# Start addresses of the matmul operands: from multiples of 64 bytes to multiples of 128 bytes

## The chip, the cores and the metric

The kernel runs on one core of a Trainium2 chip. The metric is the device time of one execution in microseconds (us). Before the change it is 881.71 us, the median of three runs (881.45 to 884.4).

## The reference

Two transformer blocks, one after the other, on 256 tokens of width 1024, all in float32:

```python
def reference(x, mem, ...):
    x = first_block(x, mem, ...)    # differential + stick-breaking attention, cross attention, MLP
    return second_block(x, ...)     # compressed/selected/window attention + dilated attention, gates, MLP

# both blocks end in an MLP of this form (d_ff = 4096)
a = jnp.square(jax.nn.relu(rms_norm(h, g_mlp) @ w_up))
h = h + a @ w_down
```

Nearly all the arithmetic is in the products with weight matrices: `w_in`, `w_out`, `w_xq`, `w_xkv`, `w_xo`, `w_up`, `w_down` of the first block and their counterparts in the second.

## The kernel before

**Layout.** Activations stay in the on-chip memory (SBUF) transposed, 128 features on the partitions and 256 tokens along the row, eight such slices to a tile: `[128, 8, 256]` float32, 8,192 bytes per partition. There are eight buffers of that size (class `c8` of `t`), and with the tiles of the MLP's hidden units (`mhl`, also 8,192 bytes) they hold every activation that a large product reads.

**Products in three parts.** Each float32 operand of a large product is split in a high and a low part of type float32r: ScalarE writes the high part (`hi = Copy(x)`) and VectorE the low one (`lo = x - hi`). `mm3` (lines 263 to 268) then issues three matmuls into the same PSUM bank: high weight with high activation (L266), low weight with high activation (L267), high weight with low activation (L268). In `gemm_t` and in the MLPs the weights are the stationary operand (128 x 128) and the activations the moving one (256 columns, 1,024 bytes per partition). In `gemm_n` (L319 to L321) it is the other way round: 128 tokens of the activation are stationary and 256 columns of weights move. `acc_add` has the same three parts in another order (L334, L335, L338). The built program has 1,544 matmuls of each of L266 to L268, 432 of each of L319 to L321 and 80 of each of L334, L335 and L338: 6,168 in all. The rest (attention scores and values, transposes) are plain float32.

**Weights.** `wunit` (line 207) brings a unit of weights with DMAs from SyncE's queue into staging buffers `wraw` and splits it piece by piece: 512 numbers per partition go to one buffer of `whi` (L232, ScalarE) and one of `wlo` (L233, VectorE). Each of the two has NPART = 8 buffers that are used in turn, and each buffer has STEP floats more than its 512:

```python
    NRAW, NPART, NP = 6, 8, 10
    STEP = 16
...
hi, lo = [self.t([P, 512 + self.STEP], tag, self.NPART, F32R, self.wp)[:, :rows * cols] ...
          for tag in ("whi", "wlo")]
```

One pair of buffers feeds 12 matmuls in a row, in `gemm_t` (two slices of 128 weight rows, two groups of 128 columns, three parts) and in the MLP's second product (`out_rows`, one weight row slice, four column groups, three parts). One turn of the MLP's loop (`mlp`, `for u in range(2, nu)`) is one unit of `w_up` (four pairs, 48 matmuls, into bank G) and one of `w_down` (four pairs, 48 matmuls, into banks Z and X): 96 matmuls and each of the eight pairs once.

**Where the operands stand.** The constants come first in memory, one tile after the other, each rounded up to 32 bytes; `gsub`, 4 bytes, is one of the first. The pool with the activations follows, then the pool of the weights. The built program's map has these start addresses (bytes within a partition):

| buffers | before | remainder |
|---|---|---|
| eight buffers of activations, `mhl` among them | 30784 + 8192 i | 64 by 1024 |
| `whi` | 194368 + 2112 i | 320, 384, 448, 0, 64, 128, 192, 256 by 512 |
| `wlo` | 211264 + 2112 i | the same eight by 512 |
| `wraw` | 169792 + 4096 i | 64 by 256 |

Rows inside a buffer begin at multiples of 512 bytes from its start. So before the change every operand of a large product starts at a multiple of 64 bytes: all activations at an odd one (64 past a multiple of 128), half of the weight buffers at an odd one and half at an even one. In the stretches that the rows below show, the pairs are used in this order (remainder by 512 of `whi` / `wlo`):

| runs of 12 that start at | pairs in turn |
|---|---|
| 300.29 to 310.15 us, first MLP | 192/192, 256/256, 128/384, 384/448, 448/0, 0/128, 64/64, 320/320 |
| 742.39 to 752.35 us, second MLP | 192/192, 0/128, 256/256, 64/64, 320/320, 128/384, 384/448, 448/0 |
| 518.45 and 519.86 us, `gemm_n` | 192/192, 256/256 |

Of the kernel before, what the change touches and what calls it, by code (L numbers as in the profile page):

```python
# [9 lines left out]
F32 = mybir.dt.float32  # L10
# [7 lines left out]
P = 128  # L18
# [116 lines left out]
class Builder:  # L135
# [66 lines left out]


    NRAW, NPART, NP = 6, 8, 10
    STEP = 16

    def wunit(self, src, j, n, dmas=1, before=None, hold_lo=None):

# [17 lines left out]
        for j0 in range(0, j, rows):  # L226
            for c0 in range(0, n, cols):
                hi, lo = [self.t([P, 512 + self.STEP], tag, self.NPART, F32R, self.wp)[:, :rows * cols].rearrange(
                    "p (r c) -> p r c", r=rows) for tag in ("whi", "wlo")]
# [200 lines left out]
    def setup(self):  # L430
        nc, I = self.nc, self.I
        nc.scalar.preload_act_table_set(MAIN_SET)
        self.ones = self.cp.tile([P, P], F32, name="ones")
        nc.vector.memset(self.ones, 1.0)

        z = self.Z()
        for _ in range(10):
            nc.tensor.matmul(z[:, 0:P], self.ones, self.ones, start=True, stop=True)
        gains = self.const("gains", [P, 7 * 8 + 1], eng=nc.scalar)
        self.xT = self.t([P, KC, T], "h")  # L440
        xv = I["xT"].rearrange("(k p) t -> p k t", p=P)
        self.first_unit = self.wcols(I["w_in"], 1536, dmas=4, before=lambda i: nc.sync.dma_start(
            self.xT[:, 2 * i:2 * i + 2], xv[:, 2 * i:2 * i + 2]))
        self.ident = self.const("ident", [P, P])
        self.g = {n: gains[:, 8 * i:8 * i + 8] for i, n in enumerate(GAINS)}
        self.gsub = self.cp.tile([P, 1], F32, name="gsub")
        nc.vector.tensor_scalar(out=self.gsub, in0=gains[:, 56:57], scalar1=1.0 - LAM_INIT, scalar2=None,
                                op0=ALU.mult)
        self.one = self.cp.tile([P, 1], F32, name="one")
        nc.vector.memset(self.one, 1.0)  # L450
        self.zero = self.cp.tile([P, 1, 1], F32, name="zero")
        nc.vector.memset(self.zero, 0.0)
        self.nones = self.cp.tile([P, P], F32, name="nones")
        nc.gpsimd.memset(self.nones, -1.0)
# [1064 lines left out]
```

## Time and profile before

| | before |
|---|---|
| three timed runs | 881.45, 881.71, 884.4 us |
| the profiled execution: its own time | 880.0 us |
| its span in the trace | 877.8 us |
| TensorE matmuls (PE) | 860.9 us busy, 98% of the span, 7,109 instructions |
| TensorE weight loads (PEld) | 828.0 us, 94% |
| VectorE (DVE) | 602.1 us, 69% |
| ScalarE (ACT) | 551.9 us, 63% |
| GpSimd (POOL) | 95.6 us, 11% |
| read from the chip's main memory | 142.46 MB, 163 GB/s over the span |

The trace gives each matmul a duration of about 0.28 us, but they are pipelined: the next one starts about 0.12 us after the one before. How fast TensorE goes is therefore read from the starts of successive matmuls, not from their durations.

### The profile page before, as it was taken

What the parts mean: (1) busy time and instruction counts of PE and PEld (TensorE: products, weight loads), DVE (VectorE), ACT (ScalarE), POOL (GpSimd) and SP (SyncE); (2) the same over time, 40 slices, a digit from 0 to 9 for tenths busy, and PEclk for the clock granted to TensorE, in tenths of its full rate; (3) what the DMA queues carried; (4) which work ended last, traced back from release to release, by engine and by line L of the source; (5) the groups of instructions that cost most, each with busy time, mean ns of one, the idle gap of its engine ahead of it and who ended that gap; (6) DMA issues with size and microseconds to landing.
All of it is one profiled execution on the core that took longest, in us unless ns stands there. A gap on an engine that the chain in (4) does not pass through costs nothing.

```text
span 877.8 us, 18311 instructions
## 1 busy us (share of the span) xinstructions
PE 860.9 (98%) x7109; PEld 828.0 (94%) x7109; DVE 602.1 (69%) x1291; ACT 551.9 (63%) x1199; POOL 95.6 (11%) x139
## 2 busy tenths in 40 slices
PE   7999999999999999999999999999988999999998
PEld 6989999999999999999998999889978999999997
DVE  7645687585597555675877786686947975555554
ACT  5769577464575555664674887877764665555551
POOL 4032100020020000000203130113410300000000
PEclk9999999999999999999999999999999999999999
DMA  9655445653466766766387354232623565666541
GB/s 312 182 183 155 143 133 157 193 171 94 144 177 181 217 192 184 229 200 205 83 256 245 121 164 125 73 86 84 213 101 96 165 211 181 189 192 187 183 136 49
DMA packets 111830, 144.68 MB, mean 165 GB/s; under 512 B 6272, under 2 KB 100096, under 8 KB 111744
## 3 DMA queue, kind: packets, MB, share of 16 engines
q1 hardware_dynamic: 111600, 143.50, 53.2%
q8 instruction: 55, 0.90, 0.4%
q14 instruction: 31, 0.25, 0.1%
q10 hardware_dynamic: 144, 0.03, 0.0%
HBM read 142.46 MB, written 1.05 MB: 163 GB/s over the span
## 4 chain that ended last, share of the span: by engine, by line
PE 92%; ACT 3%; DMA 2%; DVE 2%; issue 1%; POOL 0%; SPq 0%; ACTq 0%; DVEq 0%; POOLq 0%
PE G L266 12%; PE G L267 12%; PE G L268 12%; PE G L320 5%; PE G L321 5%; PE G L319 5%; PE Z L268 4%; PE Z L267 4%; PE Z L266 4%; PE X L266 4%; PE X L268 4%; PE X L267 4%; PE X L427 3%; DMA wraw<-w_in 2%; PE Z L627 2%; PE O L640 1%
## 5 line engine op out<-in xcount | busy, mean ns | idle before, releaser
L233 DVE TENSOR_TENSOR wlo<-wraw,whi 128x512 fp32r<-128x512 f32 (+1 forms) x512 | 348.8, 696 | 167.4 <-ACT whi L232 164.6
L232 ACT ACTIVATE whi<-wraw 128x512 fp32r<-128x512 f32 (+1 forms) x512 | 313.6, 624 | 201.6 <-PE G L268 83.6
L267 PE MATMUL G<-acth,wlo 128*128 128x256 f32 x892 | 251.2, 283 | 4.3 <-DVE wlo L233 4.3
L266 PE MATMUL G<-acth,whi 128*128 128x256 f32 x892 | 252.3, 284 | 0.6 <-DVE gm L1352 0.3
L268 PE MATMUL G<-actl,whi 128*128 128x256 f32 x892 | 249.0, 283 | 0.0
L267 PEld LDWEIGHTS G<-acth,wlo 128*128 128x128 f32 x892 | 168.4, 189 | 6.0 <-DVE wlo L233 5.1
L266 PEld LDWEIGHTS G<-acth,whi 128*128 128x128 f32 x892 | 168.8, 189 | 2.6 <-issue 0.8
L268 PEld LDWEIGHTS G<-actl,whi 128*128 128x128 f32 x892 | 167.0, 189 | 0.3
L319 PE MATMUL G<-whi,acth 128*128 128x256 f32 x400 | 114.0, 286 | 0.0
L320 PE MATMUL G<-wlo,acth 128*128 128x256 f32 x400 | 114.0, 285 | 0.0
L321 PE MATMUL G<-whi,actl 128*128 128x256 f32 x400 | 114.0, 285 | 0.0
L320 PEld LDWEIGHTS G<-wlo,acth 128*128 128x128 f32 x400 | 75.5, 189 | 1.4 <-issue 0.8
L319 PEld LDWEIGHTS G<-whi,acth 128*128 128x128 f32 x400 | 75.4, 189 | 1.4 <-ACT whi L232 0.4
L321 PEld LDWEIGHTS G<-whi,actl 128*128 128x128 f32 x400 | 75.5, 189 | 1.0 <-issue 0.8
L266 PE MATMUL X<-mhl,whi 128*128 128x256 f32 x240 | 67.6, 282 | 0.5 <-DVE mt L1471 0.5
L268 PE MATMUL Z<-mhl,whi 128*128 128x256 f32 x240 | 67.5, 281 | 0.0
L268 PE MATMUL X<-mhl,whi 128*128 128x256 f32 x240 | 67.4, 281 | 0.0
L266 PE MATMUL Z<-mhl,whi 128*128 128x256 f32 x240 | 67.3, 281 | 0.0
L267 PE MATMUL X<-mhl,wlo 128*128 128x256 f32 x240 | 67.3, 280 | 0.0
L267 PE MATMUL Z<-mhl,wlo 128*128 128x256 f32 x240 | 67.3, 280 | 0.0
L266 PEld LDWEIGHTS X<-mhl,whi 128*128 128x128 f32 x240 | 45.3, 189 | 0.7 <-DVE mt L1471 0.7
L654 ACT ACTIVATE p<-p,mx 128x256 f32<-128x256 f32 x88 | 39.0, 446 | 10.2 <-DVE mx L647 6.1
(393 smaller groups left out, 1523.0 us busy)
## 6 DMA issues: line engine op xcount, KB each, us to landing
wraw<-w_up SPq DMA_DIRECT2D x64, 512.0 KB, 3.9
wraw<-w_down SPq DMA_DIRECT2D x64, 512.0 KB, 3.6
wraw<-w_in SPq DMA_DIRECT2D x42, 512.0 KB, 4.6
wraw<-w_dil SPq DMA_DIRECT2D x18, 512.0 KB, 4.1
wraw<-w_xkv SPq DMA_DIRECT2D x16, 512.0 KB, 3.7
wraw<-w_out SPq DMA_DIRECT2D x16, 512.0 KB, 3.7
wraw<-w_in SPq DMA_DIRECT2D x22, 256.0 KB, 5.5
wraw<-w_xq SPq DMA_DIRECT2D x8, 512.0 KB, 3.8
```

The costliest lines, as they stand in the source:

```text
L232: nc.scalar.activation(hi, r, AF.Copy)
L233: i = nc.vector.tensor_tensor(out=lo, in0=r, in1=hi, op=ALU.subtract)
L266: mm(out, w[0], x[0], start=first, stop=False, skip_group_check=True)
L267: mm(out, w[1], x[0], start=False, stop=False, skip_group_check=True)
L268: mm(out, w[0], x[1], start=False, stop=last, skip_group_check=True)
L319: mm(outs[tt], x[0][:, k, ts_], w[0], start=first, stop=False, skip_group_check=True)
L320: mm(outs[tt], x[0][:, k, ts_], w[1], start=False, stop=False, skip_group_check=True)
L321: mm(outs[tt], x[1][:, k, ts_], w[0], start=False, stop=(k == KC - 1), skip_group_check=True)
L427: self.mark = self.nc.tensor.transpose(out, in_, self.ident[:n, :n])
L627: i = mm(z[:, 0:256], q[rs, P:T], k[rs, 0:256], start=True, stop=True)
L640: mm(po[rs], v0[a], pts[a][:, 0:256], start=False, stop=last, skip_group_check=True)
L654: self.nc.scalar.activation(s[:, sl], s[:, sl], AF.Exp, scale=-1.0, bias=m[:, i:i + 1], accum_out=sums[:, i:i + 1])
```

## The change

Two edits. `STEP` goes from 16 to 32 floats, so the buffers of `whi` and `wlo` stand 2,176 bytes apart instead of 2,112. And `gsub` becomes the first column of a tile of 17 floats, which takes 96 bytes instead of 32 and so moves all that is allocated after it by 64 bytes.

```diff
     NRAW, NPART, NP = 6, 8, 10
-    STEP = 16
+    STEP = 32
...
-        self.gsub = self.cp.tile([P, 1], F32, name="gsub")
+
+        self.gsub = self.cp.tile([P, 17], F32, name="gsub")[:, 0:1]
         nc.vector.tensor_scalar(out=self.gsub, in0=gains[:, 56:57], scalar1=1.0 - LAM_INIT, scalar2=None,
```

The built program's map after the change:

| buffers | after | remainder |
|---|---|---|
| eight buffers of activations | 30848 + 8192 i | 128 by 1024 |
| `whi` | 194432 + 2176 i | 384, 0, 128, 256, 384, 0, 128, 256 by 512 |
| `wlo` | 211840 + 2176 i | the same by 512 |
| `wraw` | 169856 + 4096 i | 128 by 256 |

All 6,168 large matmuls now read both operands from multiples of 128 bytes. The pairs in use are 384/384 (twice), 128/128, 0/0, 256/256, 256/0, 0/128 and 128/256. No instruction is added or removed, and the order on every engine, with the waits, is the same as before, row for row; only line numbers below the second edit grow by one.

## Rows read from the trace of the kernel before

**Rows 1.** The page: TensorE's busy time; its granted clock in 40 slices.
```profile
PE 860.9 (98%) x7109; PEld 828.0 (94%) x7109; DVE 602.1 (69%) x1291; ACT 551.9 (63%) x1199; POOL 95.6 (11%) x139
...
PEclk9999999999999999999999999999999999999999
```

**Rows 2.** The page: the chain that ended last, shares by engine.
```profile
PE 92%; ACT 3%; DMA 2%; DVE 2%; issue 1%; POOL 0%; SPq 0%; ACTq 0%; DVEq 0%; POOLq 0%
```

**Rows 3.** The waits of PE, longest in total: us, times, longest.
```profile
PE G L267 <- DVE wlo L233: 4.3, 4, 1.5
PE X L427 <- ACT pt L669: 1.8, 1, 1.8
```

**Rows 4.** Windows: length; busy PE, PEld, DVE, ACT, POOL; PEclk, DMA share, GB/s.
```profile
240.00:430.00 190.00, 189.85 (x1611) 189.59 (x1610) 132.31 (x233) 113.38 (x203) 10.62 (x13) 1.00 0.64 191
430.00:640.00 210.00, 208.78 (x1738) 190.93 (x1738) 163.60 (x473) 157.49 (x439) 42.88 (x56) 1.00 0.49 149
690.00:872.00 182.00, 182.00 (x1538) 181.94 (x1537) 114.63 (x174) 97.23 (x165) 6.32 (x7) 1.00 0.53 164
```

**Rows 5.** Timeline of PE, first MLP: first matmul of each run of 12.
```profile
300.29 0.28 PE L266 MATMUL G<-acth,whi 128*128 128x256 f32 x1
...
301.71 0.28 PE L266 MATMUL G<-acth,whi 128*128 128x256 f32 x1
...
303.12 0.28 PE L266 MATMUL G<-acth,whi 128*128 128x256 f32 x1
...
304.48 0.28 PE L266 MATMUL Z<-mhl,whi 128*128 128x256 f32 x1
...
305.90 0.28 PE L266 MATMUL Z<-mhl,whi 128*128 128x256 f32 x1
...
307.34 0.28 PE L266 MATMUL Z<-mhl,whi 128*128 128x256 f32 x1
...
308.71 0.28 PE L266 MATMUL Z<-mhl,whi 128*128 128x256 f32 x1
...
310.15 0.28 PE L266 MATMUL G<-acth,whi 128*128 128x256 f32 x1
...
311.59 0.28 PE L266 MATMUL G<-acth,whi 128*128 128x256 f32 x1
```

**Rows 6.** Timeline of PE, second MLP: first matmul of each run of 12.
```profile
742.39 0.27 PE L266 MATMUL Z<-mhl,whi 128*128 128x256 f32 x1
...
743.81 0.28 PE L266 MATMUL Z<-mhl,whi 128*128 128x256 f32 x1
...
745.24 0.28 PE L266 MATMUL Z<-mhl,whi 128*128 128x256 f32 x1
...
746.65 0.28 PE L266 MATMUL Z<-mhl,whi 128*128 128x256 f32 x1
...
748.08 0.28 PE L266 MATMUL G<-acth,whi 128*128 128x256 f32 x1
...
749.52 0.28 PE L266 MATMUL G<-acth,whi 128*128 128x256 f32 x1
...
750.93 0.28 PE L266 MATMUL G<-acth,whi 128*128 128x256 f32 x1
...
752.35 0.28 PE L266 MATMUL G<-acth,whi 128*128 128x256 f32 x1
...
753.76 0.27 PE L266 MATMUL Z<-mhl,whi 128*128 128x256 f32 x1
```

**Rows 7.** Timeline of PE in `gemm_n`: first matmul of each run of 12.
```profile
518.45 0.28 PE L319 MATMUL G<-whi,acth 128*128 128x256 f32 x1
...
519.86 0.28 PE L319 MATMUL G<-whi,acth 128*128 128x256 f32 x1
...
521.23 0.28 PE L319 MATMUL G<-whi,acth 128*128 128x256 f32 x1
```

## The prediction

> **What bounds the kernel now.** [...] In the two MLPs (240 to 430 us and 690 to 872 us) PE and PEld are both busy all the time, with VectorE at 70% and 63%; only in the second block's attention (430 to 640 us) are VectorE and ScalarE near 75 to 78% [rows 4]. So what counts is how soon one matmul follows the other, and that is in the timeline of PE.
>
> The reader should take the first matmul of each run of 12 and subtract. In the first MLP the eight runs of one loop turn take 1.42, 1.41, 1.36, 1.42, 1.44, 1.37, 1.44 and 1.44 us, together 11.30 us [rows 5]. In the second they take 1.42, 1.43, 1.41, 1.43, 1.44, 1.41, 1.42 and 1.41 us, together 11.37 us [rows 6]. That is 22.67 us for 192 matmuls, 118.1 ns each. All have the same shape, clock and moving address (64 past a multiple of 1,024). What differs is the weight pair. I call an operand odd that stands 64 bytes past a multiple of 128, even one that stands on it.
>
> Both odd: pairs 64/64 and 320/320 take 1.44 and 1.44 us in the first MLP, 1.43 and 1.44 in the second; pair 192/192 takes 1.42 in both [rows 5, 6]. Activation odd, weights even: 128/384, 0/128 and 256/256 take 1.36, 1.37 and 1.41 us in the first MLP, but 1.41, 1.43 and 1.41 in the second [rows 5, 6]. With the roles exchanged in `gemm_n`, weights moving and activation stationary, the odd pair takes 1.41 us and the even pair 1.37 [rows 7]. So start addresses do set the pace, between 113.3 ns (1.36 us / 12) and 120.0 ns (1.44 / 12), and both operands matter.
>
> **The change part by part.** It adds and removes no instruction and moves none in any queue. The larger `gsub` tile and the larger buffers cost memory alone. The staging buffers move by 64 bytes too, and the splits on ScalarE and VectorE read and write at the new addresses; their cover is TensorE's time, of which VectorE leaves 30% and 37% in the MLPs [rows 4]. Both bounds there are near nothing: a gain is hidden, and a loss would have to exceed that slack to be seen. Without this cover, each per cent on VectorE in the MLPs would be a per cent of its 132 and 115 us busy [rows 4]. The plain float32 matmuls keep shape and number; I count them at nothing, since no row parts them by address.
>
> That leaves 6,168 matmuls of which all operands become even. Before: both odd about 3,100 times (all odd pairs, and parts of the mixed ones), one of them even otherwise. The trace has no matmul of this kind with both even, so I bound it from both sides. The upper bound is the both-odd run, 1.44 us: if only the distance between the operands matters, nothing has been gained. The lower bound takes the best step seen, 1.44 to 1.36 when one operand becomes even, a second time: 1.28 us, 106.7 ns per matmul. I take 1.36 us, the least for 12 that the trace shows at all: both-even should be no worse than the better one-even stretch, and nothing shows the second step. The one-even stretches of the second MLP (1.41 to 1.43) I read as follows: each stands next to a both-odd run there [rows 6], while in the first MLP the 1.36 us of 128/384 come after 256/256 and not after an odd pair [rows 5]. After the change there is no odd run left to come from.
>
> The sum: 16 runs at 1.36 us are 21.76 us, 113.3 ns per matmul; 118.1 less 113.3 is 4.74 ns (unrounded), times 6,168 is 29.2 us. Not all of it reaches the end. The attention stretch of the second block has 1,224 of these matmuls, 5.8 us of the gain, and with VectorE and ScalarE at 75 to 78% there [rows 4] I let half of it turn into waits for them: 2.9 us. In the MLPs what is late next would be the weight split on VectorE, 132 of 190 us [rows 4], still far from the end. So 26.3 us come off. The profiled execution took 880.0 us for a span of 877.8 us, so 2.2 us lie around it and stay; 880.0 - 26.3 = 853.7. The median of the three runs is 1.7 us above that execution, so I forecast 855.4 us.
>
> **The rivals.** *Only the distance counts (slower).* Suppose that it is not where an operand stands but how far the two streams that TensorE reads stand apart, by 256 bytes, for instance because they share interleaved parts of the memory. The rows fit this too: distance 0 takes longest (64/64 and 320/320 with the activation at 64: 1.44), distance 128 is 192/192 (1.42), and distances 64 and 192 are the even pairs (1.36 to 1.43) [rows 5, 6]. In `gemm_n` the 1.37 us belong to distance 64 again, with the parts exchanged [rows 7]. After the change all distances are 0 or 128. Of the eight pairs three have both parts at distance 0 (384/384 twice, 128/128 against 128), three both at 128 (0/0, 256/256, 256/0), two are mixed: 3 x 1.44 + 3 x 1.42 + 2 x 1.43 = 11.44 us per turn against 11.335 before, the mean of the two turns. That is 1.09 ns per matmul, 6.7 us over 6,168, nearly all of it on the path since TensorE never waits in the MLPs: 881.7 + 6.7 = 888.4 us. It decides as soon as the new runs take more than 1.426 us on average. For it speaks that 64/64 and 192/192 differ at all, which evenness doesn't explain; against it, that 256/256 and 128/384 share a value in the second MLP though their distances differ [rows 6]. Were every run at distance 0, 1.44, it would be 893.6 us.
>
> *The second step comes as well (deep).* If each odd operand costs its own 0.08 us per run, both-even takes 1.28 us. That is 11.4 ns per matmul less, 70.3 us; with a tenth lost to waits 63 us, and the time about 818 us. For it speaks that 1.44 is as far above 1.36 as 1.36 above 1.28, against it that the one-even stretches of 1.41 to 1.43 show no clean sum of two costs. [...]
>
> *Nothing changes.* If 64 bytes are fine already and the differences between runs have another source that stays (the number of buffers between a pair, say), the time stays at 881.7 us. Against it stand the runs 1.36 and 1.44 of the same loop turn [rows 5]. [...] That the change doesn't do what it says is no rival here: the built program's map has all 6,168 pairs at multiples of 128.
>
> **How the numbers follow.** The forecast, runs between 1.33 and 1.39 us, has 0.36; by the same sum, with a tenth lost, it spans 842 to 869 us. Runs at 1.39 to 1.405, still a gain of over 0.5%, have 0.04. The deep case has 0.15, no change 0.12, the distance 0.33. A measurement of this kernel can tell about 0.5%, 4.4 us, from no change. Faster is 0.36 + 0.04 + 0.15 = 0.55, same 0.12, slower 0.33. The range goes from 842 us, leaving out the deep case, to 890 us, which holds the distance rival but for its end where all runs take 1.44 (0.05): 0.80 inside.
>
> **What would show it.** In the profile of the changed kernel the starts of a run of 12 in either MLP answer at once: 1.36 us and flat is the forecast; 1.44 for pairs 384/384 and 128/128 beside 1.42 for 0/0 and 256/256 is the distance; 1.28 is the second step. One turn of the loop should take 10.9 us, not 11.44. The waits of PE for `wlo` should grow by a few us if the forecast holds. The forecast is wrong if two runs that differ only in the distance of their operands differ as much as odd and even do now.

## The result and the profile after

The changed kernel takes 886.84 us, the median of four runs (885.85 to 888.19), against 881.58 us for the kernel before (881.43 to 884.4). The ratio is 1.0053 with a 95% interval from 1.0034 to 1.0072: half a per cent slower, where a gain of 26 us was forecast. What came true is the rival in which only the distance between the operands counts (the stationary operand's start address less the moving one's, by 256 bytes): it gave 888.4 us.

The page of the changed kernel answers [rows 1, 2]: busy time by engine, the granted clock in 40 slices, and the chain that ended last.

```profile
PE 867.4 (98%) x7109; PEld 834.6 (94%) x7109; DVE 602.6 (68%) x1291; ACT 552.1 (62%) x1199; POOL 96.3 (11%) x139
...
PEclk9999999999999999999999999999999999999999
...
PE 92%; DVE 3%; DMA 2%; ACT 2%; issue 1%; POOL 0%; SPq 0%; ACTq 0%; DVEq 0%; POOLq 0%
```

TensorE is busy 6.5 us longer (860.9 before), and the span grows by 6.1 us, from 877.8 to 883.9. The other engines are where they were to within 0.7 us, the granted clock is again 9 tenths or more in every slice (mean 0.999, 1.000 before), and the chain is as much TensorE's as before. The waits of TensorE in the changed kernel (us in total, times, longest) are those of [rows 3] to 0.1 us:

```profile
PE G L267 <- DVE wlo L233: 4.4, 4, 1.5
PE X L427 <- ACT pt L670: 1.8, 1, 1.8
```

So the loss lies between one matmul and the next. The timeline of PE in the changed kernel, first MLP, the first matmul of each run of 12 (start, duration, engine, line, operation); it answers [rows 5]:

```profile
300.08 0.28 PE L266 MATMUL Z<-mhl,whi 128*128 128x256 f32 x1
...
301.51 0.28 PE L266 MATMUL G<-acth,whi 128*128 128x256 f32 x1
...
302.95 0.28 PE L266 MATMUL G<-acth,whi 128*128 128x256 f32 x1
...
304.39 0.28 PE L266 MATMUL G<-acth,whi 128*128 128x256 f32 x1
...
305.81 0.28 PE L266 MATMUL G<-acth,whi 128*128 128x256 f32 x1
...
307.23 0.28 PE L266 MATMUL Z<-mhl,whi 128*128 128x256 f32 x1
...
308.65 0.28 PE L266 MATMUL Z<-mhl,whi 128*128 128x256 f32 x1
...
310.08 0.28 PE L266 MATMUL Z<-mhl,whi 128*128 128x256 f32 x1
...
311.52 0.28 PE L266 MATMUL Z<-mhl,whi 128*128 128x256 f32 x1
```

Subtract: 1.43, 1.44, 1.44, 1.42, 1.42, 1.42, 1.43 and 1.44 us, one turn of 11.44 us where it was 11.30. The pairs in this stretch are, in the same order, 384/384, 384/384, 128/128 (distance 0), 256/256, 0/0 (distance 128), 0/128, 128/256 (mixed) and 256/0 (distance 128). No run takes 1.36 us any more. The second MLP, same view:

```profile
742.15 0.28 PE L266 MATMUL G<-acth,whi 128*128 128x256 f32 x1
...
743.59 0.28 PE L266 MATMUL G<-acth,whi 128*128 128x256 f32 x1
...
745.01 0.28 PE L266 MATMUL G<-acth,whi 128*128 128x256 f32 x1
...
753.59 0.28 PE L266 MATMUL G<-acth,whi 128*128 128x256 f32 x1
```

1.44, then 1.42, and 11.44 us for the whole turn, against 11.37 [rows 6]. A mean over the whole trace takes all successive large matmuls with 256 moving columns that start less than 140 ns apart, 5,877 pairs in either kernel (48 matmuls of `gemm_n` move 292 columns and are left out). From start to start it goes from 118.04 to 119.03 ns; 0.99 ns times 6,168 is 6.1 us, which is the growth of the span.

Sorted by distance, the trace of before has 119.5 ns at 0, 118.1 at 128, 117.2 at 64 and 192 together, each distance about a quarter of the matmuls. The change took the 64 and the 192 away, the two that were quickest.

### The profile page after: what moved, and what is told of

Read it like the earlier page. It is cut to its first block, busy times and chain, and to the rows that moved or that the text cites. A ratio compares the mean times of both kernels' runs of the same rounds, so it can differ in the third digit from the quotient of the medians.

```text
span 883.9 us, 18311 instructions
## 1 busy us (share of the span) xinstructions
PE 867.4 (98%) x7109; PEld 834.6 (94%) x7109; DVE 602.6 (68%) x1291; ACT 552.1 (62%) x1199; POOL 96.3 (11%) x139
## 4 chain that ended last, share of the span: by engine, by line
PE 92%; DVE 3%; DMA 2%; ACT 2%; issue 1%; POOL 0%; SPq 0%; ACTq 0%; DVEq 0%; POOLq 0%
PE G L266 12%; PE G L267 12%; PE G L268 12%; PE G L320 5%; PE G L321 5%; PE G L319 5%; PE Z L268 4%; PE Z L267 4%; PE Z L266 4%; PE X L266 4%; PE X L267 4%; PE X L268 4%; PE X L427 3%; DMA wraw<-w_in 2%; PE Z L628 2%; PE O L641 1%
## 5 line engine op out<-in xcount | busy, mean ns | idle before, releaser
L266 PEld LDWEIGHTS X<-mhl,whi 128*128 128x128 f32 x240 | 45.4, 189 | 0.7 <-DVE mt L1472 0.7
L268 PEld LDWEIGHTS X<-mhl,whi 128*128 128x128 f32 x240 | 45.6, 190 | 0.0
```

The costliest lines, as they stand in the source:

```text
L266: mm(out, w[0], x[0], start=first, stop=False, skip_group_check=True)
L268: mm(out, w[0], x[1], start=False, stop=last, skip_group_check=True)
```

## Experiments: one edit at a time

Of the two edits the first, alone, leaves every operand at an odd place (64 past a multiple of 128) and gives the distances of the changed kernel, 0 and 128:

```diff
-    STEP = 16
+    STEP = 32
```

> One half of the change alone: STEP = 32, gsub as before. Activations stay 64 bytes past a multiple of 1,024, all weight buffers are 64 past a multiple of 128, so every operand is odd, at distances 0 and 128 (by 256) from its partner, the same distances as in the changed kernel. Theory 'distance' (the pace depends on the distance between the two operands of a matmul by 256 bytes, wherever they stand): the time of the changed kernel, 886.8 us, within 1 us; a turn of the MLP loop takes 11.44 us. Rival 'place' (each operand costs by its own address, odd worse than even): clearly over the changed kernel, whose operands are all even: every run of 12 at 1.42 to 1.44 us and 888 to 894 us only if even operands were worth something there.

Measured: 888.54 us (887.13 to 890.21), ratio 1.0076 [1.0055, 1.0097]. The timeline of PE in this kernel, first MLP, first matmuls of the first, second and third run of a turn and of the run behind the turn:

```profile
300.09 0.28 PE L266 MATMUL Z<-mhl,whi 128*128 128x256 f32 x1
...
301.52 0.28 PE L266 MATMUL G<-acth,whi 128*128 128x256 f32 x1
...
302.96 0.28 PE L266 MATMUL G<-acth,whi 128*128 128x256 f32 x1
...
311.53 0.28 PE L266 MATMUL Z<-mhl,whi 128*128 128x256 f32 x1
```

1.43, 1.44 and again 11.44 us for the turn: with everything at odd places this is the changed kernel over again, and the mean over all is 119.03 ns in both. The time is 1.7 us above the changed kernel's, where at most 1 us was expected; at the same mean granted clock, 0.998, an execution of the one took 887.13 us and one of the other 886.91. The second edit alone moves the activations to multiples of 128 and keeps the weights' eight phases, so that all four distances remain:

```diff
-        self.gsub = self.cp.tile([P, 1], F32, name="gsub")
+        self.gsub = self.cp.tile([P, 17], F32, name="gsub")[:, 0:1]
```

> The other half alone: 64 bytes in front of the activations (17 floats for gsub), STEP = 16. Activations stand at 128 by 1,024, weight buffers at all eight multiples of 64 by 512, distances 0, 64, 128 and 192 in equal shares as in the kernel before. Theory 'distance': the time of the kernel before, 881.6 us, within 1 us. Rival 'place': activations are even as in the changed kernel and half of the weights odd, so it is no longer the mix of the kernel before; if the even activations are what made the changed kernel slower, at least 886 us; if even operands help, under 880 us.

Measured: 881.67 us (879.49 to 885.81, ten runs), ratio 1.0001 [0.9986, 1.0016], mean 118.00 ns. This is the kernel before, with half of its pairs now even on both sides. In these kernels it makes no difference whether an operand is even: all odd equals all even, if the distances are equal. The whole 5 us belong to STEP, because STEP sets the distances.

## Experiments: one distance for all

Four kernels have STEP = 0, so that all eight pairs of buffers are 2,048 bytes apart and have one distance. Three of them also have a tile ahead of the weights' pool that sets it:

```diff
-    STEP = 16
+    STEP = 0
...
+        self.wpad = self.wp.tile([P, 16], F32, name="wpad")
```

That is for 64 bytes; 48 floats give 192, 32 floats give 128, and without the tile the distance is 0. In `gemm_n`, where the roles are exchanged, 64 becomes 192 and the reverse. 96 of the 6,168 matmuls read their weights from other buffers (`wbh`, `wbl`), which stand with the activations, and stay at distance 0 in every kernel. Some kernels from here on ran once. A single time says little, since the kernel before took 879.75 to 884.32 us in 19 runs; there the reading rests on the pace in the trace.

> STEP = 0: weight buffers 2,048 bytes apart, all operands 64 past a multiple of 256, distance 0 everywhere. Theory 'distance': every run of 12 takes 1.44 us, flat 120 ns; (120.0 - 118.1) x 6,168 = 11.9 us over the kernel before, 893 us. Rival 'place': all operands odd as in e1_step, so the same time as e1_step.

Measured for distance 0: 892.21 us (891.86 to 893.55), ratio 1.0120 [1.0102, 1.0138]. That is 3.7 us above the kernel with the first edit alone, although all operands of both are odd. The timeline of PE shows flat runs of 1.44 us, 120.0 ns for each matmul:

```profile
300.11 0.28 PE L266 MATMUL Z<-mhl,whi 128*128 128x256 f32 x1
...
301.55 0.28 PE L266 MATMUL Z<-mhl,whi 128*128 128x256 f32 x1
...
302.99 0.28 PE L266 MATMUL G<-acth,whi 128*128 128x256 f32 x1
```

> STEP = 0 and 128 bytes in front of the weight pool: weights at 192 by 256, activations at 64, distance 128 everywhere. Theory 'distance': no other distance in the row before it, so the runs of 12 should repeat the 1.42 us of pairs 0/0 and 256/256 of the changed kernel; 118.5 to 119 ns per matmul, 885 us. Rival 'place': all operands odd as in e0_d0 and e1_step, and so their 888 to 892 us.

Measured for distance 128: 884.37 us, one run beside 881.92 for the kernel before; runs of 1.42 to 1.43 us, mean 118.74 ns over all.

> STEP = 0 and a tile of 64 bytes in front of the weight pool that nothing uses: activations at 64, weight buffers at 128 by 256, distance 64 in gemm_t and the MLPs (4,824 matmuls), 192 in gemm_n (1,248), where the roles are exchanged. Theory 'distance': runs of 12 at 1.36 us in the MLPs once the run before is of the same kind: 4.7 ns x 4,824 = 22.9 us less, about 858 us; if the runs get stuck at the 1.41 us that pairs of this distance take in the second MLP of the kernel before, 878 us. Rival 'place': weights even, activations odd: at best the mean of the one-even runs of the kernel before (1.40 us), 875 us.

Measured for distance 64: 879.21 us (877.93 to 880.93, ten runs), ratio 0.9967 [0.9954, 0.9981]. The 858 us hoped for were missed by 21 us; what came is the other branch of the expectation, runs stuck at 1.41 us and 878 us. The timeline of PE:

```profile
300.87 0.28 PE L267 MATMUL G<-acth,whi 128*128 128x256 f32 x1
...
302.29 0.28 PE L267 MATMUL G<-acth,whi 128*128 128x256 f32 x1
...
303.70 0.28 PE L267 MATMUL Z<-mhl,whi 128*128 128x256 f32 x1
```

1.42 and 1.41 us (1.413 each, before rounding): 117.75 ns, flat, and only 1 in 10 matmuls at 113.3.

> STEP = 0 and 192 bytes in front of the weight pool: weights at 0 by 256, activations at 64, distance 192 in gemm_t and the MLPs, 64 in gemm_n. Theory 'distance', with the pace also set by how the two streams fell into step before: runs of 12 flat at 1.41 us as with distance 64, which locked at 1.413 us, so about 879 us. Rival 'place': weights and activations stand as in e3_d64 (weights even, activations odd), the same 879 us; the two part only if distance 192 has a pace of its own, 1.36 us (858 us) or 1.42 and more.

Measured for distance 192: 878.43 us, one run. The timeline of PE in the first MLP, and then in `gemm_n`, whose distance here is 64:

```profile
300.29 0.28 PE L267 MATMUL G<-acth,whi 128*128 128x256 f32 x1
...
301.70 0.28 PE L267 MATMUL G<-acth,whi 128*128 128x256 f32 x1
...
519.08 0.28 PE L320 MATMUL G<-whi,acth 128*128 128x256 f32 x1
...
520.44 0.28 PE L320 MATMUL G<-whi,acth 128*128 128x256 f32 x1
```

The MLP goes at 1.41 us; this stretch of `gemm_n` goes at 1.36. So a distance of 64 or 192 has two paces, 117.75 and 113.3 ns, each flat for many runs, and both better than the 118.74 and 120.0 of the other two distances. Which of the two it is the distance alone doesn't say. The trace of before has this too, once one looks for it: the pair 128/384, both parts at distance 64, takes 1.36 us in the first MLP [rows 5] and 1.41 in the second [rows 6].

A finer map has STEP = 8, which gives distances at all multiples of 32:

> STEP = 8: weight buffers 2,080 bytes apart, so the eight pairs stand at distances that are multiples of 32 bytes, 0 to 224. A look at finer steps. Theory 'distance': a smooth course from 1.44 us at 0 over about 1.41 at 64 and 192 to 1.42 at 128, with 32, 96, 160 and 224 between their neighbours; about 882 us. Rival: what counts is whether an operand begins at a multiple of 64 bytes at all; then the pairs at 32 past take clearly longer than all others, 1.45 us or more, and the time is over 890 us.

Measured: 883.77 us, one run. The timeline of PE, first MLP; the runs' distances are, for the high parts, 192, 224, 160, 32, 64, 96, 128 and 0, for the low ones 192, 224, 32, 64, 96, 160, 128 and 0:

```profile
301.33 0.28 PE L266 MATMUL G<-acth,whi 128*128 128x256 f32 x1
...
302.70 0.28 PE L266 MATMUL G<-acth,whi 128*128 128x256 f32 x1
...
304.10 0.28 PE L266 MATMUL G<-acth,whi 128*128 128x256 f32 x1
...
305.52 0.28 PE L266 MATMUL Z<-mhl,whi 128*128 128x256 f32 x1
...
306.94 0.28 PE L266 MATMUL Z<-mhl,whi 128*128 128x256 f32 x1
...
308.38 0.28 PE L266 MATMUL Z<-mhl,whi 128*128 128x256 f32 x1
...
309.80 0.28 PE L266 MATMUL Z<-mhl,whi 128*128 128x256 f32 x1
...
311.24 0.28 PE L266 MATMUL G<-acth,whi 128*128 128x256 f32 x1
...
312.67 0.28 PE L266 MATMUL G<-acth,whi 128*128 128x256 f32 x1
```

1.37, 1.40, 1.42, 1.42, 1.44, 1.42, 1.44 and 1.43 us. The 1.45 us and more of the rival appear nowhere. An address 32 past a multiple of 64 shows no cost of its own: distance 224 takes 1.40 us, between the values of its neighbours. The other distances that aren't multiples of 64 occur in mixed pairs only, and these take 1.42 to 1.44 us.

## Experiments: the better of the two paces

If a run's pace depends on what it follows, alternating distances might do what one distance doesn't. The next kernel leaves the activations at 64 and has STEP = 32 with the pad of 64 bytes, so three of the eight pairs are at 64, three at 192, and two have their parts at different distances:

```diff
-    STEP = 16
+    STEP = 32
...
+        self.wpad = self.wp.tile([P, 16], F32, name="wpad")
```

> STEP = 32 and 64 bytes in front of the weight pool: as the changed kernel with every weight buffer 64 bytes further from the activations, so the distances alternate between 64 and 192 where the changed kernel has 0 and 128. Theory 'distance': no run at 1.42 to 1.44 us is left; a change of distance from one run to the next may bring the pace of 1.36 us (in the kernel before, 192 followed by 64 did), so between 866 and 879 us. Rival 'place': all weights even, activations odd, as in e3_d64: 879 us.

Measured: 864.2 us, one run beside 881.92, somewhat below the expected range. Except for a few runs near the start of each MLP, all runs of both are flat at 1.36 us. In `gemm_n` most stay at the other pace: the means there are 116.1 ns at 64 and 117.9 at 192.

The test that bears on the case itself is the changed kernel with only this pad added. Its activations stand at even places, its weights all at odd ones, and the distances are 64 and 192 where they were 0 and 128:

> The changed kernel (STEP = 32, 17 floats for gsub) with 64 bytes more in front of the weight pool: activations even (128 by 256), all weights odd, the distances 64 and 192 of e6_alt at other places. Theory 'distance': the time of e6_alt, 864 us, within 2 us, and 1.36 us per run of 12 in the MLPs. Rival 'place': the parts are exchanged against e6_alt (there weights even, activations odd), and the one odd operand is the one that is read in another role; no reason for the same time, and nothing below 875 us if the 864 us came from even weights.

Measured: 862.26 us (860.72 to 862.6), ratio 0.9775 [0.9755, 0.9796] to the kernel before, beside which it ran; it beats both kernels. Its page (busy time) and its timeline of PE in the first MLP, the first three runs of a turn and the run behind it:

```profile
PE 844.3 (98%) x7109; PEld 811.2 (94%) x7109; DVE 600.9 (70%) x1291; ACT 550.8 (64%) x1199; POOL 97.8 (11%) x139
```

```profile
301.22 0.28 PE L267 MATMUL Z<-mhl,whi 128*128 128x256 f32 x1
...
302.58 0.28 PE L267 MATMUL Z<-mhl,whi 128*128 128x256 f32 x1
...
303.94 0.28 PE L267 MATMUL Z<-mhl,whi 128*128 128x256 f32 x1
...
312.10 0.28 PE L267 MATMUL Z<-mhl,whi 128*128 128x256 f32 x1
```

1.36, 1.36 us and a turn of 10.88 us, on TensorE's side a gain of 23 us over the changed kernel (867.4 to 844.3) from 64 bytes of unused memory. The mean over all is 114.62 ns; (118.04 - 114.62) times 6,168 is 21.1 us, and 882.80 - 862.26 = 20.5 us were measured.

Two kernels ask what sets off the better pace. Both have STEP = 0; `whi` and `wlo` are allocated apart, with 128 bytes between them, so that within every pair the two parts have different distances. In one the high parts stand at 64 and the low at 192 (pad of 16 floats), in the other the reverse (48 floats):

```diff
-                hi, lo = [self.t([P, 512 + self.STEP], tag, self.NPART, F32R, self.wp)...
+                hi = self.t([P, 512 + self.STEP], "whi", self.NPART, F32R, self.wp)...
+                if not getattr(self, "wgap", None):
+                    self.wgap = self.wp.tile([P, 32], F32, name="wgap")
+                lo = self.t([P, 512 + self.STEP], "wlo", self.NPART, F32R, self.wp)...
```

> STEP = 0, all high weight parts at distance 64, all low ones at 192 (128 bytes between the two groups of buffers). What brings the pace of 1.36 us in e6_alt, where distance 64 alone gave 1.413 us? Theory 'mixed pair': the switch between 64 and 192 inside a pair does it; then every run is at 1.36 us, about 860 us. Rival 'change of run': it takes a change of distance from one run to the next; here all runs are alike, so 1.41 us and 879 us.

> The same with the two exchanged: high parts at distance 192, low ones at 64. Theory 'mixed pair': 1.36 us per run in one of the two orders at least, about 860 us. Rival 'change of run': 1.41 us, 879 us.

Measured, one run each beside 882.8 for the kernel before: 864.07 us with the high parts at 64, 878.45 us with the high parts at 192. The timeline of PE, first the one, then the other:

```profile
301.18 0.28 PE L271 MATMUL Z<-mhl,whi 128*128 128x256 f32 x1
...
302.54 0.28 PE L271 MATMUL Z<-mhl,whi 128*128 128x256 f32 x1
```

```profile
300.64 0.28 PE L271 MATMUL G<-acth,whi 128*128 128x256 f32 x1
...
302.06 0.28 PE L271 MATMUL G<-acth,whi 128*128 128x256 f32 x1
```

1.36 us against 1.42. That the parts differ in distance is therefore not enough. Nor does the order of the distances inside the triple of matmuls decide it alone: the second kernel has both paces in the same kind of product. Its timeline of PE a little earlier:

```profile
243.27 0.28 PE L271 MATMUL G<-acth,whi 128*128 128x256 f32 x1
...
244.63 0.28 PE L271 MATMUL G<-acth,whi 128*128 128x256 f32 x1
...
247.42 0.28 PE L271 MATMUL G<-acth,whi 128*128 128x256 f32 x1
...
248.84 0.28 PE L271 MATMUL G<-acth,whi 128*128 128x256 f32 x1
```

The run from 243.27 us takes 1.36 us, the one from 247.42 us 1.42, and that pace the rest of the first MLP's loop keeps; the second MLP changes in the same way between 711 and 714 us. And in this kernel's `gemm_n`, where the high parts are at 64 and the low ones at 192, the mean is 117.9 ns and not 113.3. What brings the better pace and what ends it isn't settled by these runs.

## Why the prediction was wrong, point by point

**What bounds the kernel: right [rows 1 to 4].** TensorE's pace is the whole of it. In all these kernels the time follows the mean from start to start (862.26 us at 114.62 ns, 881.67 at 118.00, 884.37 at 118.74, 886.84 at 119.03), and the traces of the changed kernel and of the best one show VectorE and ScalarE busy within 2 us of before (602.6 and 552.1 us, 600.9 and 550.8 us, against 602.1 and 551.9). The staging buffers' move and the splits at new addresses cost nothing that shows, as assumed.

**The step that failed: what the 64 bytes stand for.** From [rows 5 to 7] the prediction read that a run gets quicker when one of its operands is even. But in the kernel before, every activation is odd at the same place, so "the weights are even" and "the distance is 64 or 192" are one and the same set of runs; the rows couldn't part the two readings. The first edit alone did: odd everywhere, at distances 0 and 128, it takes 888.5 us like the changed kernel with all even, and the second edit alone, with even activations but the old distances, takes 881.7 us like the kernel before. It is the distance. The staging buffers, which the pad moves too, aren't the cause: `STEP` alone leaves them where they were, and already costs what the whole change does.

**The value taken for it.** "Both even" had no row in the trace, and 1.36 us was chosen between 1.44 and 1.28 as the least seen. The upper bound, "if only the distance between the operands matters, nothing has been gained", was the nearer one: 1.430 us on average in the first MLP's turn. With 119.03 ns in the place of 113.3 the term of 29.2 us less becomes 6.1 us more.

**The reading of the second MLP: half right.** The prediction put the 1.41 to 1.43 us of the even pairs there down to the neighbouring odd runs [rows 6]. That more than a run's own pair counts is borne out: the same distance of 64 takes 1.36 us in the changed kernel with the pad, and 1.41 us where all pairs are at 64. The run just ahead doesn't decide it either, since with the pad a pair at 64 behind another at 64 goes at 1.36 us too. And the reading was used to argue that the slow values would go, and not to doubt that evenness was their cause.

**The rivals.** The distance rival was worked out to the run: 11.44 us per turn, and 11.44 were measured in both MLPs; 6.7 us in all, of which the span shows 6.1. It had a chance of 0.33. What was put against it, that two pairs at different distances share a value in the second MLP, is no objection once a distance of 64 has two paces. Its own bound for all runs at distance 0, 893.6 us, came out as 892.2. The deep case (1.28 us) appears in no kernel: the best flat pace of any is 113.3 ns. "Nothing changes" falls, though narrowly: the interval of the ratio leaves 1 out.

**The late term** was never tested by the changed kernel, but the best kernel bears on it: at nearly the forecast pace in the MLPs its waits for `wlo` don't grow (1.9 us, 4.4 in the changed kernel). Of the 6.9 us that it lacks to the forecast of 855.4 us, by estimate about 5 lie where the weights move (`gemm_n`): a mean of 117.2 ns instead of 113.3 for 1,248 matmuls.

## What to carry to other kernels

When rows suggest that a property of one operand sets the pace, check what else is the same in every such row: here evenness and distance were one set, and a forecast on either was a guess until an edit parted them. Where TensorE runs back to back and loads new weights for every matmul, as in this kernel, look at the two operands' addresses against each other by 256 bytes and not at the alignment of either; a step between buffers and 64 unused bytes that make the distances 64 and 192 were worth 2.2% here. A pattern that the trace doesn't contain (both even) deserves the bound that adds no new mechanism as its likeliest value.

## What the runs showed of the hardware

- **Distance, not alignment.** For these matmuls (stationary 128 x 128, 256 columns moving, float32r, a new stationary operand each time, mean granted clock 0.992 to 1.000 in the profiled executions) the pace goes by the stationary address less the moving one, modulo 256: 120.0 ns at 0, 118.7 at 128, 117.75 or 113.3 at 64 and 192. Of the pairs at 0, 64/64 and 320/320 stand 256 bytes apart and both take 1.44 us in the first MLP [rows 5]. Moving both streams together by 64 bytes changes nothing (119.03 ns twice; 118.04 and 118.00). The kernel at distance 0 and the one at 64 differ by the pad alone and take 892.21 and 879.21 us. Weight loads and matmuls run side by side (828.0 and 860.9 us busy in the 877.8 us of the kernel before). Why the distance of the two operands counts, by shared parts of the memory as the rival supposed or otherwise, no run shows.
- **Two stable paces at one distance.** At 64 and 192 the stream falls into 117.75 or 113.3 ns and keeps it for many runs. With high parts at 64 and low at 192 both MLP loops keep the better one, and with pairs at 64 and pairs at 192 mixed nearly all runs of the MLPs go at it; with the reverse order a stretch at the better one changes to 1.42 us a run without any change of distance (one run each). What decides, and why `gemm_n` seldom gets there, is open.
